# A transformer trunk on one core: the third unit's first two products moved ahead of those that read S2, and the last token tile's chain written first

## The chip, the cores and the metric

The kernel runs on one core of a Trainium2 chip. The metric is the device time of one execution in microseconds (us). The core has TensorE (PE, matrix products), VectorE (DVE), ScalarE (ACT), GpSimd (POOL) and SyncE (SP), which here only issues transfers. Each engine runs its own instructions in a fixed order; they wait for each other by semaphores.

## The reference

One layer on 1024 tokens of width 1024, in float32:

```python
h    = x @ w_in                              # columns: pool | q | k | v | forget gate
pool = scale * GroupLinear(trailing_mean(u) - u)
attn = forgetting_attention(q, k, v, f)      # 8 heads, causal
x    = layer_norm(ALPHA * x + concat(pool, attn) @ w_out)
hid  = square(relu(x @ w_mlp1))              # 1024 -> 4096
x    = layer_norm(ALPHA * x + hid @ w_mlp2)  # 4096 -> 1024
```

## The kernel before, in words

**Precision.** Every operand of a product is split into a hi part (a cast on ScalarE, L71) and a lo part (VectorE subtracts hi from the source, L72). A product is then three matmuls: hi by hi, hi by lo, lo by hi.

**Stages.** First the projections, the pooling and the attention. Then, for token tiles t = 0 to 7 of 128 tokens, the projection by `w_out` (L743 to L745, two banks of 512 columns), the residual (L750) and the norm (`Norm`, with L513 and L516 as its two passes over the tile and a store of the result, L517). Then w_mlp1 in 16 units of 256 columns, and last w_mlp2 in steps (L918).

**Seven products instead of eight.** The product with w_mlp1 cuts x1 (the norm's output, transposed, [channels, tokens]) into four blocks: A11 and A12 are the two halves of the channels for tokens 0 to 511, A21 and A22 those for tokens 512 to 1023. A Strassen-Winograd scheme needs sums of blocks: S1 = A21 - A22, S2 = S1 - A11, S3 = A11 - A21, S4 = A12 + S2. On the weights' side a unit has B11, B21, and B22, T1 to T4, made of sums. The seven products of a unit are `p1` (A11 by B11), `p2` (A12 by B21), `p6` (S2 by T2), `p5` (S1 by T1), `p7` (S3 by T3), `p3` (S4 by B22) and `p4` (A22 by T4): 12 matmuls each (L575), four channel tiles by three hi/lo pairs.

**Where the blocks come from.** `x1_transposed(t, y)` turns one token tile: eight transposes on TensorE (L551). For t below 4 it splits straight into A11 and A12 and keeps a raw copy in `R0[j]`, j = t % 4. For t of 4 and more it makes the differences: ScalarE copies A22, VectorE subtracts three times (L566, L567, L568), POOL adds (L569). The tile just normed is turned while the next one is projected, so tile 7 is turned after the first unit's products have begun. `block(name, src)` splits all four token tiles of a block into two B tiles.

**A unit's weights.** Two loads of 512 KB from w_mlp1, `load_f` (B11 and B21, L592) and `load_g` (L596). `split_f` makes B11 and B21, `sums` makes T1 to T4 in place, `split_t2`, `split_t14` and `split_t3b` split them. `u1` is a copy of `p1`'s bank (L635), `ra` the sum with `p2` (L642), `rb` made behind `p7` (L658) before `p4` adds on to the same bank. Behind `p4` come ReLU and square, sums of the results (`sa`, `sb`, L673 to L678), their splits (L690, L691) and stores to `hid_dram` (L693, L706, issued by POOL).

**Memory and order.** SBUF tiles come from pools shared by a tag: S has 3 tiles, U 2, B 14, Q 10, A 9. The eight split w_out tiles are B tiles, free when the last projection has read them. PSUM has eight banks in a cycle of tags. A tile that is asked for waits until one of its pool is free. A planner in the language's framework fixes each engine's order ahead of the run: among what it deems ready, what stands first in the text goes first. So the text's order is a priority. The first two units, `first` and `second`, run side by side in an order written out by hand (L760 to L808), and `third` is drawn into it; from there on a loop interleaves one unit with the one before it.

Of the kernel before, what the change touches and what calls it, by code (L numbers as in the profile page):

```python
# [8 lines left out]
F32 = mybir.dt.float32  # L9
# [3 lines left out]
ALU = mybir.AluOpType  # L13

P = 128
S = 1024
D = 1024
NT = S // P
# [18 lines left out]
def trunk(ctx, tc, xT, xn, wuqk, wvf, bf, poolw, pscale, wout, g1, b1, w1, w2, g2, b2, out):  # L37
# [5 lines left out]
    nc = tc.nc  # L43
# [7 lines left out]
    def slot(tag, shape, dt=F32R):  # L51
        uid[0] += 1
        return sb.tile([P] + list(shape), dt, tag=tag, bufs=NBUF[tag], name=f"{tag}{uid[0]}")
# [9 lines left out]
    def bank(tag=None):  # L63
        uid[0] += 1
        if tag is None:
            tag = CYCLE[rr[0] % 8]
            rr[0] += 1
        return ps.tile([P, CH], F32, tag=tag, bufs=PBUF[tag], name=f"{tag}{uid[0]}")

    def split(hi, lo, src):  # L70
        nc.scalar.copy(hi, src)  # L71
        nc.vector.tensor_tensor(lo, src, hi.bitcast(F32), ALU.subtract)  # L72
# [8 lines left out]
    def three(dst, a, b, first, last):  # L81

        nc.tensor.matmul(dst, a[0], b[0], start=first, stop=False)  # L83
        nc.tensor.matmul(dst, a[0], b[1], start=False, stop=False)  # L84
        nc.tensor.matmul(dst, a[1], b[0], start=False, stop=last)  # L85
# [97 lines left out]
    for t in range(4, NT):  # L183
        for half in range(2):
            b = bank()[:, 0:VW]
# [273 lines left out]
    H = KT // 2  # L459
# [78 lines left out]
    R0, R1, A22, raw22 = {}, {}, {}, {}  # L538

    def split_to(blk, j, src):  # L540
        js = slice(j * P, (j + 1) * P)
        hi, lo = (a[:, :, js] for a in A[blk])
        split(hi, lo, src)

    def x1_transposed(t, y):
        j = t % 4
        tps = []
        for half in range(2):
            tp = bank()
            for k in range(4):  # L550
                nc.tensor.transpose(tp[:, k * P : (k + 1) * P], y[:, (4 * half + k) * P : (4 * half + k + 1) * P], ident)  # L551
            tps.append(tp.rearrange("p (k t) -> p k t", k=4))
        if t < 4:
            R0[j] = slot("A", [2, H, P], F32)
            for half in range(2):
                split_to(("A11", "A12")[half], j, tps[half])
                nc.scalar.copy(R0[j][:, half], tps[half])
            return

        tag = "A" if j < 2 else "Q"  # L560
        R1[j] = r = slot(tag, [2, H, P], F32)
        if j % 2 == 0:
            raw22[j // 2] = slot(tag, [2, H, P], F32)
        A22[j] = a22 = raw22[j // 2][:, j % 2]
        nc.scalar.copy(a22, tps[1])
        nc.vector.tensor_tensor(r[:, 0], R0[j][:, 0], tps[0], ALU.subtract)  # L566
        nc.vector.tensor_tensor(r[:, 1], tps[0], a22, ALU.subtract)  # L567
        nc.vector.tensor_tensor(R0[j][:, 0], r[:, 1], R0[j][:, 0], ALU.subtract)  # L568
        nc.gpsimd.tensor_tensor(R0[j][:, 1], R0[j][:, 1], R0[j][:, 0], ALU.add)  # L569


    def product(dst, b, a, first):
# [10 lines left out]
    class Unit:  # L583
# [19 lines left out]
        def split_f(self, tag="Q"):  # L603
            if tag == "B":
                w = slot("B", [2, 2, H, P])
                hi, lo = w[:, 0], w[:, 1]
            else:
                hi, lo = slot(tag, [2, H, P]), slot(tag, [2, H, P])
            self.keep(("B11", "B21"), hi, lo, self.f)

        def sums(self, eng=None):

            eng = eng or nc.vector
            f, g = self.f, self.g
            self.t2 = slot("U", [H, P], F32)
            eng.tensor_tensor(f[:, 0], f[:, 0], g[:, 0], ALU.add)
            eng.tensor_tensor(self.t2, g[:, 1], f[:, 0], ALU.add)
            eng.tensor_tensor(f[:, 1], self.t2, f[:, 1], ALU.add)
            eng.tensor_tensor(g[:, 0], g[:, 1], g[:, 0], ALU.add)
# [94 lines left out]
    last = None  # L714
    for m in range(4):
        mh = []
        for half in range(2):
            mf = slot("S", [4, 256], F32)
            nc.sync.dma_start(mf, mix_dram[m, :, 4 * half : 4 * half + 4, :])
            if half:  # L720
                rb = slot("S", [NPAIR, 256], F32)
                for e in range(2):
                    rows = rin_dram[e::2, m * 256 : (m + 1) * 256].rearrange("(o p) t -> o p t", o=1)
                    nc.sync.dma_start(rb[e * HD : (e + 1) * HD], rows.to_broadcast([HD, NPAIR, 256]))
                nc.vector.tensor_tensor(mf, mf, rb, ALU.mult)
            hi, lo = slot("Q", [4, 256]), slot("Q", [4, 256])
            split(hi, lo, mf)
            mh.append((hi, lo))
        for t in (2 * m, 2 * m + 1):
            ts_ = slice((t % 2) * P, (t % 2 + 1) * P)  # L730
            xt = slot("A", [D], F32)
            nc.sync.dma_start(xt, xn[t])
            if t == NT - 1:
                for un in units[:2]:
                    un.load_f()
                    un.split_f("B")
                    if un.u == 0:
                        un.load_g()
                        un.sums(nc.gpsimd)
            yp = [bank() for n in range(2)]  # L740
            for n, part in enumerate(yp):
                ns = slice(n * CH, (n + 1) * CH)
                for k in range(KT):  # L743
                    a = mh[k // 4]
                    three(part, (a[0][:, k % 4, ts_], a[1][:, k % 4, ts_]), (wo[k][0][:, ns], wo[k][1][:, ns]), k == 0, k == KT - 1)  # L745
            if last is not None:
                x1_transposed(*last)
            nm = Norm(xt, gam, bet, x1_dram[t])
            for i, c in enumerate(nm.cols):
                nc.vector.scalar_tensor_tensor(xt[:, c], xt[:, c], ALPHA, yp[i], ALU.mult, ALU.add)  # L750
                nm.stats(i)
            nm.on_vector()
            last = (t, xt)

    def block(name, src):
        A[name] = (slot("B", [H, CH]), slot("B", [H, CH]))
        for j in range(4):
            split_to(name, j, src(j))

    first, second, third = units[:3]  # L760
    second.load_g("A")
    for un in (first, second):
        un.p1()
        un.p2()
    x1_transposed(*last)
    block("S2", lambda j: R0[j][:, 0])
    first.split_t2()
    first.split_t14()
    second.sums()
    second.split_t2()  # L770
    first.p6()
    second.p6()
    block("S1", lambda j: R1[j][:, 1])
    block("S3", lambda j: R1[j][:, 0])
    second.split_t14()
    first.p5()
    second.p5()
    third.load_f()
    block("S4", lambda j: R0[j][:, 1])
    first.split_t3b()  # L780
# [2 lines left out]
    first.p7()  # L783
    second.p7()
    first.p3()
    third.split_f()
    third.load_g()
    second.p3()
    third.sums()
    first.p4()  # L790
    first.sums_s()
    third.split_t2()
    third.p1()
    first.out_r()
    third.split_t14()
    first.out_s()
    second.p4()
    third.p2()
    units[3].load_f()
    units[3].split_f()  # L800
    second.sums_s()
# [302 lines left out]
```

## Time and profile before

| | |
|---|---|
| median of 3 runs | 1059.61 us (1059.41 to 1061.12) |
| the profiled execution | 1059.77 us, its span in the trace 1058.0 us |
| granted TensorE clock, mean over the span | 0.991 |
| TensorE busy | 1023.5 us, 97% |
| VectorE, ScalarE, POOL busy | 761.4 us (72%), 513.6 us (49%), 118.9 us (11%) |

Matmuls are pipelined: the length of one in the trace is longer than the distance to the next, and their ends are modelled. So spacing is read from starts. The granted clock is 1.00 at 2.4 GHz and 0.50 at 1.2 GHz. An idle time is put down to the event that came last before the engine went on.

### The profile page before, as it was taken

The page shows a single profiled execution, that of the slowest core. Times are in us where ns is not written, and L with a number is a line of the kernel's source. Part 1 is how long each engine was busy: PE and PEld are TensorE (multiplying, and loading weights), DVE is VectorE, ACT ScalarE, POOL GpSimd, SP SyncE. Part 2 cuts the span into 40 slices and gives each one's busy share as a digit, 9 for nine tenths or more (in the row PEclk, how much of TensorE's full clock was granted, in tenths as well). Part 3 has the DMA queues.
Part 4 walks back from the last instruction along what each step waited for, and adds up shares of the span by engine and source line. Part 5 has one row for each costly group of instructions (what it writes and reads, how often), then busy time and mean ns, then how long its engine had stood idle before and what let it go on. Part 6 is the DMA issues. An engine that isn't in the chain of part 4 may idle for free.

```text
span 1058.0 us, 14056 instructions
## 1 busy us (share of the span) xinstructions
PE 1023.5 (97%) x5006; PEld 846.8 (80%) x5006; DVE 761.4 (72%) x1297; ACT 513.6 (49%) x822; POOL 118.9 (11%) x187
## 2 busy tenths in 40 slices
PE   8999999999989999899999999999899999999994
PEld 8988787888768888688888888888678888888883
DVE  4576677777896898879878788788686576566446
ACT  4423665565773323567676766668431221122053
POOL 0000000000000021112112122120100000000056
PEclk9999999999999999899999999999999999999998
DMA  6303311021446542238757567575799888868673
GB/s 220 103 27 107 98 50 43 19 64 39 135 152 165 180 152 80 76 132 314 273 219 277 222 257 267 214 268 191 288 296 326 281 271 287 274 217 258 196 224 119
DMA packets 111510, 195.28 MB, mean 185 GB/s; under 512 B 9224, under 2 KB 77640, under 8 KB 111440
## 3 DMA queue, kind: packets, MB, share of 16 engines
q1 hardware_dynamic: 95456, 136.19, 39.5%
q0 software_dynamic: 15984, 58.20, 14.2%
q8 instruction: 39, 0.64, 0.2%
q14 instruction: 31, 0.25, 0.1%
HBM read 126.65 MB, written 67.70 MB: 184 GB/s over the span
## 4 chain that ended last, share of the span: by engine, by line
PE 55%; issue 22%; DVE 8%; DMA 6%; POOL 5%; ACT 3%; SPq 0%; POOLq 0%; DVEq 0%; ACTq 0%
PE s L918 14%; PE pv L918 7%; POOL hid_dram L693 4%; PE pv L384 3%; PE mm L85 2%; PE mm L83 2%; DMA S<-rin_dram 2%; PE mm L84 2%; PE s L83 2%; PE s L85 2%; PE s L84 2%; PE mm L918 2%; PE s L575 2%; PE pt L918 2%; PE pt L83 2%
## 5 line engine op out<-in xcount | busy, mean ns | idle before, releaser
L71 ACT CAST B<-S 128x1024 fp32r<-128x1024 f32 (+1 forms) x94 | 80.1, 869 | 177.8 <-DMA S<-in_w_dram 82.8
L918 PE MATMUL s<-B,Q 128*128 128x512 f32 x549 | 134.1, 391 | 2.6 <-DVE rt L505 2.2
L72 DVE TENSOR_TENSOR B<-S,B 128x1024 fp32r<-128x1024 f32 (+1 forms) x94 | 93.5, 1004 | 46.2 <-ACT B L71 46.0
L918 PEld LDWEIGHTS s<-B,Q 128*128 128x128 f32 x549 | 103.3, 189 | 25.4 <-DVE rt L505 2.6
L575 PE MATMUL s<-B,Q 128*128 128x512 f32 x504 | 121.5, 395 | 0.4 <-ACT B L71 0.4
L575 PEld LDWEIGHTS s<-B,Q 128*128 128x128 f32 x504 | 96.0, 191 | 21.4 <-ACT B L71 0.9
L71 ACT CAST Q<-S 128x1024 fp32r<-128x1024 f32 x53 | 55.5, 1050 | 66.9 <-PE s L575 17.2
L72 DVE TENSOR_TENSOR Q<-S,Q 128x1024 fp32r<-128x1024 f32 x53 | 64.6, 1221 | 25.4 <-ACT Q L71 25.2
L575 PE MATMUL mm<-B,Q 128*128 128x512 f32 x324 | 77.6, 389 | 0.0
L693 POOL DMA_DIRECT2D hid_dram<-A x90 | 48.3, 540 | 234.9 <-ACT A L690 198.0
L575 PEld LDWEIGHTS mm<-B,Q 128*128 128x128 f32 x324 | 60.7, 188 | 13.0 <-DVE Q L72 0.4
L575 PE MATMUL pt<-B,Q 128*128 128x512 f32 x288 | 68.7, 389 | 0.0
L918 PE MATMUL pv<-B,Q 128*128 128x512 f32 x273 | 67.2, 390 | 0.0
L384 PE MATMUL pv<-A,B 128*128 128x256 f32 x320 | 61.6, 297 | 4.9 <-ACT A L369 3.3
L384 PEld LDWEIGHTS pv<-A,B 128*128 128x128 f32 x320 | 49.0, 188 | 21.3 <-ACT A L369 10.0
L575 PEld LDWEIGHTS pt<-B,Q 128*128 128x128 f32 x288 | 54.1, 188 | 11.2
L370 DVE TENSOR_TENSOR A<-pt,A 128x512 fp32r<-128x512 f32 (+1 forms) x80 | 49.2, 634 | 16.4 <-ACT A L369 15.8
L918 PEld LDWEIGHTS pv<-B,Q 128*128 128x128 f32 x273 | 51.3, 188 | 10.8
L347 ACT ACTIVATE A<-A,nm 128x128 f32<-128x128 f32 (+3 forms) x64 | 49.7, 777 | 20.7 <-DVE nm L345 20.4
L691 DVE TENSOR_TENSOR A<-A,A 128x1024 f32<-128x1024 f32 x45 | 53.4, 1219 | 0.0
L83 PE MATMUL mm<-B,B 128*128 128x512 f32 x120 | 51.7, 431 | 0.0
L369 ACT CAST A<-pt 128x512 fp32r<-128x512 f32 (+1 forms) x80 | 41.8, 539 | 16.9 <-PE pt L368 16.2
(395 smaller groups left out, 2214.9 us busy)
## 6 DMA issues: line engine op xcount, KB each, us to landing
hid_dram<-A POOLq DMA_DIRECT2D x105, 512.0 KB, 4.1
Q<-hid_dram SPq DMA_DIRECT2D x139, 256.0 KB
S<-in_w_dram SPq DMA_DIRECT2D x63, 512.0 KB
A<-hid_dram SPq DMA_DIRECT2D x41, 256.0 KB
S<-in_wuqk_dram SPq DMA_DIRECT2D x12, 512.0 KB
Q<-hid_dram SPq DMA_DIRECT2D x44, 128.0 KB
A<-ncf_dram SPq DMA_DIRECT2D x8, 512.0 KB
S<-in_wout_dram SPq DMA_DIRECT2D x8, 512.0 KB
```

Of the source, the lines that this page charges most:

```text
L71: nc.scalar.copy(hi, src)
L72: nc.vector.tensor_tensor(lo, src, hi.bitcast(F32), ALU.subtract)
L83: nc.tensor.matmul(dst, a[0], b[0], start=first, stop=False)
L84: nc.tensor.matmul(dst, a[0], b[1], start=False, stop=False)
L85: nc.tensor.matmul(dst, a[1], b[0], start=False, stop=last)
L347: nc.scalar.activation(pt[:, :nk], pt[:, :nk], AF.Exp, bias=nm, scale=-1.0, accum_out=rsum[h][:, i : i + 1])
L370: nc.vector.tensor_tensor(tt[:, 1, ev], tp[:, ev], tt[:, 0, ev].bitcast(F32), ALU.subtract)
L384: nc.tensor.matmul(ov, V[j][:, h].rearrange("p s d -> p (s d)"), tt[:, s, a:b], start=(j == 0 and s == 0), stop=(j == 2 * m + 1 and s == 1),)
L575: nc.tensor.matmul(dst, b[x][:, k], A[a][y][:, k], start=first and k == 0 and i == 0, stop=k == H - 1 and i == 2, skip_group_check=not first,)
L691: nc.vector.tensor_tensor(x, x, hi.bitcast(F32), ALU.subtract)
L693: nc.gpsimd.dma_start(hid_dram[self.u, :, i, AT[name] : AT[name] + 2 * CH], part.rearrange("p q n t -> p (q n t)"))
L918: nc.tensor.matmul(dst, h[:, p_], w[q_], start=first and u == self.us[0] and j == 0, stop=u == self.us[-1] and j == 2, skip_group_check=no ...
```

## The change

`x1_transposed` makes S2 of a tile in `r[:, 0]` from the first difference (L567's) and, for the last tile, splits it right there; S3 goes to `R0[j][:, 0]`. For the last tile the norm now stands in the text ahead of the transposing of tile 6. `third` gets its own early load of its first weight block into a B tile (`early_f`) and a split into another, in place of `split_f` later; `load_f` stays for the sums. The order written out by hand is rearranged: second's `p1`, S2 of three tiles, the turning of tile 7, second's `p2`, then third's `p1` and `p2`, then the products with S2.

```diff
--- before.py
+++ after.py
@@ -563,10 +563,12 @@
             raw22[j // 2] = slot(tag, [2, H, P], F32)
         A22[j] = a22 = raw22[j // 2][:, j % 2]
         nc.scalar.copy(a22, tps[1])
-        nc.vector.tensor_tensor(r[:, 0], R0[j][:, 0], tps[0], ALU.subtract)
         nc.vector.tensor_tensor(r[:, 1], tps[0], a22, ALU.subtract)
-        nc.vector.tensor_tensor(R0[j][:, 0], r[:, 1], R0[j][:, 0], ALU.subtract)
-        nc.gpsimd.tensor_tensor(R0[j][:, 1], R0[j][:, 1], R0[j][:, 0], ALU.add)
+        nc.vector.tensor_tensor(r[:, 0], r[:, 1], R0[j][:, 0], ALU.subtract)
+        if t == NT - 1:
+            split_to("S2", j, r[:, 0])
+        nc.vector.tensor_tensor(R0[j][:, 0], R0[j][:, 0], tps[0], ALU.subtract)
+        nc.gpsimd.tensor_tensor(R0[j][:, 1], R0[j][:, 1], r[:, 0], ALU.add)
 
 
     def product(dst, b, a, first):
@@ -607,6 +609,13 @@
             else:
                 hi, lo = slot(tag, [2, H, P]), slot(tag, [2, H, P])
             self.keep(("B11", "B21"), hi, lo, self.f)
+
+        def early_f(self):
+
+            raw = slot("B", [2, H, P], F32)
+            w = slot("B", [2, 2, H, P])
+            nc.sync.dma_start(raw.rearrange("p b k f -> p (b k) f"), w1[2 * self.u])
+            self.keep(("B11", "B21"), w[:, 0], w[:, 1], raw)
 
         def sums(self, eng=None):
 
@@ -743,38 +752,45 @@
                 for k in range(KT):
                     a = mh[k // 4]
                     three(part, (a[0][:, k % 4, ts_], a[1][:, k % 4, ts_]), (wo[k][0][:, ns], wo[k][1][:, ns]), k == 0, k == KT - 1)
-            if last is not None:
+            if last is not None and t < NT - 1:
                 x1_transposed(*last)
             nm = Norm(xt, gam, bet, x1_dram[t])
             for i, c in enumerate(nm.cols):
                 nc.vector.scalar_tensor_tensor(xt[:, c], xt[:, c], ALPHA, yp[i], ALU.mult, ALU.add)
                 nm.stats(i)
             nm.on_vector()
+            if t == NT - 1:
+                x1_transposed(*last)
             last = (t, xt)
 
-    def block(name, src):
+    def block(name, src, n=4):
         A[name] = (slot("B", [H, CH]), slot("B", [H, CH]))
-        for j in range(4):
+        for j in range(n):
             split_to(name, j, src(j))
 
     first, second, third = units[:3]
     second.load_g("A")
-    for un in (first, second):
-        un.p1()
-        un.p2()
+    third.early_f()
+    first.p1()
+    first.p2()
+    first.split_t2()
+    second.p1()
+
+    block("S2", lambda j: R1[j][:, 0], 3)
     x1_transposed(*last)
-    block("S2", lambda j: R0[j][:, 0])
-    first.split_t2()
-    first.split_t14()
+    second.p2()
+    third.p1()
+    third.p2()
+    first.p6()
     second.sums()
     second.split_t2()
-    first.p6()
     second.p6()
+    first.split_t14()
     block("S1", lambda j: R1[j][:, 1])
-    block("S3", lambda j: R1[j][:, 0])
+    first.p5()
     second.split_t14()
-    first.p5()
     second.p5()
+    block("S3", lambda j: R0[j][:, 0])
     third.load_f()
     block("S4", lambda j: R0[j][:, 1])
     first.split_t3b()
@@ -783,19 +799,16 @@
     first.p7()
     second.p7()
     first.p3()
-    third.split_f()
     third.load_g()
     second.p3()
     third.sums()
     first.p4()
     first.sums_s()
     third.split_t2()
-    third.p1()
     first.out_r()
     third.split_t14()
     first.out_s()
     second.p4()
-    third.p2()
     units[3].load_f()
     units[3].split_f()
     second.sums_s()
```

## Rows read from the trace of the kernel before

**Rows 1.** The page, part 1: busy us (share of the span), instructions.

```profile
PE 1023.5 (97%) x5006; PEld 846.8 (80%) x5006; DVE 761.4 (72%) x1297; ACT 513.6 (49%) x822; POOL 118.9 (11%) x187
```

**Rows 2.** Waits of TensorE, 434 to the end: us in all, times, longest.

```profile
PE mm L918 <- ACT B L71: 2.4, 1, 2.4
...
PE pv L918 <- ACT A L926: 1.5, 1, 1.5
```

**Rows 3.** Waits of TensorE, 360 to 440.

```profile
PE pv L575 <- ACT B L71: 3.7, 1, 3.7
```

**Rows 4.** Windows of 2 us: busy times, granted clock, share and GB/s of DMA.

```profile
430.00:432.00 2.00, 0.00 (x0) 0.00 (x0) 2.00 (x4) 1.53 (x2) 0.00 (x0) 1.00 0.00 0
...
434.00:436.00 2.00, 1.71 (x4) 1.11 (x5) 2.00 (x4) 0.75 (x2) 2.00 (x1) 0.50 0.18 33
```

**Rows 5.** Timeline of TensorE: start, us, engine, line, operation, count, idle before.

```profile
428.31 0.60 PE L551 MATMUL s<-ident,A 128*128 128x128 f32 x4
...
434.29 8.14 PE L575 MATMUL s<-B,Q 128*128 128x512 f32 x24 [0.41 <-ACT B L71]
...
469.50 5.60 PE L575 MATMUL s<-B,Q 128*128 128x512 f32 x24
```

**Rows 6.** The chain that ended last, 355 to 485: start, us, what.

```profile
360.52 3.35 DMA S<-in_w_dram
...
420.30 2.72 PE pt L575 x12
...
444.92 2.97 PE mm L575 x12
```

**Rows 7.** Timeline of VectorE, 364 to 485.

```profile
384.00 0.68 DVE L750 SCALAR_TENSOR_TENSOR A<-A,pt 128x512 f32<-128x512 f32 x1
...
388.84 1.41 DVE L516 SCALAR_TENSOR_TENSOR A<-A,rt,Q 128x512 f32<-128x512 f32 x2
...
417.43 0.68 DVE L750 SCALAR_TENSOR_TENSOR A<-A,pt 128x512 f32<-128x512 f32 x1
...
421.76 2.38 DVE L513 SCALAR_TENSOR_TENSOR A<-A,mv,Q 128x512 f32<-128x512 f32 x2
...
426.17 1.41 DVE L516 SCALAR_TENSOR_TENSOR A<-A,rt,Q 128x512 f32<-128x512 f32 x2
...
433.50 1.22 DVE L72 TENSOR_TENSOR Q<-S,Q 128x1024 fp32r<-128x1024 f32 x1
434.64 0.68 DVE L72 TENSOR_TENSOR B<-A,B 128x512 fp32r<-128x512 f32 x1
```

**Rows 8.** A window of 20 us among the units.

```profile
540.00:560.00 20.00, 20.00 (x90) 16.57 (x89) 16.40 (x21) 13.68 (x17) 4.76 (x10) 1.00 0.67 257
```

**Rows 9.** Timeline of ScalarE, 364 to 485.

```profile
412.41 1.14 ACT L71 CAST B<-A 128x512 fp32r<-128x512 f32 x2 [4.49 <-PE pt L84]
...
465.80 1.05 ACT L690 CAST A<-A 128x1024 fp32r<-128x1024 f32 x1
...
469.72 1.03 ACT L690 CAST A<-A 128x1024 fp32r<-128x1024 f32 x1
```

**Rows 10.** Timeline of SyncE's queue, 340 to 485.

```profile
416.94 0.33 SPq L596 DMA_DIRECT2D A<-in_w_dram  x1
426.94 0.99 SPq L517 DMA_DIRECT2D x_dram<-A  x2
```

**Rows 11.** Timeline of POOL, 364 to 485.

```profile
433.75 5.12 POOL L569 TENSOR_TENSOR A<-A 128x512 f32<-128x512 f32 x1 [10.82 <-DVE A L568]
467.17 0.71 POOL L693 DMA_DIRECT2D hid_dram<-A  x1 [28.30 <-ACT A L690]
```

**Rows 12.** Timeline of VectorE, 484 to 545.

```profile
484.60 0.68 DVE L658 TENSOR_TENSOR A<-Q,s 128x512 f32<-128x512 f32 x1
```

**Rows 13.** A window of 10 us.

```profile
470.00:480.00 10.00, 10.00 (x46) 8.29 (x45) 10.00 (x14) 6.58 (x10) 2.67 (x5) 1.00 0.99 356
```

**Rows 14.** Transfers, 400 to 520: KB each, median us from issue to landing.

```profile
hid_dram<-A POOLq DMA_DIRECT2D x25, 512.0 KB, 4.3
```

## The prediction

> **What bounds the kernel now.** I read the page first [rows 1]: TensorE is busy 97% of the span. At such a share a change pays only where TensorE stands still or runs slowly, so the next view is its waits, and after that the windows of the stage that the diff touches.
>
> Behind the 435th us no wait of TensorE is above 2.4 us, and all are at steps (L918) of a later stage [rows 2]. In the stretch of the change one stands out, 3.7 us on a hi copy of ScalarE (L71) [rows 3]. The 2 us windows show both halves of that hole [rows 4]: no matmul from 430 to 432, and a granted clock of 0.50 from 434 to 436, which is the lower level, 1.2 GHz, although TensorE is busy again. Before the clock fell the engine had stood idle for almost 4 us.
>
> The timeline of TensorE says what is on either side [rows 5]. Four products (`p1` and `p2` of first and second, 12 matmuls each, 2.72 us [rows 6]) run to 428.31, then the eight transposes of the last token tile until about 429.2, then nothing but a lone matmul until 434.29. From there to 469.50, where the third unit's `p6` starts, lie 12 products: `p6 p5 p7 p3 p4` of the first two units and the third's `p1` and `p2`. Counted: 12 x 2.72 = 32.6, and 0.9 for the transposes, is 33.5; the stretch from 428.31 to 469.50 took 41.2. The excess is 7.7 us. It is made of the idle part (429.2 to 434.29, less one matmul of 0.23: 4.9), of 24 matmuls in 8.14 instead of 2 x 2.72 (2.7), and of 0.25 in second's `p5`, 2.97 instead of 2.72.
>
> What is late at 434.29 is S2 of the last tile. Its chain in VectorE's timeline [rows 7]: the norm's end (the L516 pair from 426.17), transposes, then L566, L567 and L568 in a queue without a gap (VectorE is busy 2.00 of 2 in [rows 4]), a cast on ScalarE, and the lo half at 434.64, behind T1 and T4 of the first unit (433.50, 1.14 us).
>
> **Does the time later on follow this stage?** From 480 to about 740 TensorE is busy 20.00 of 20 in every window; one stands in [rows 8]. A unit is 7 products, 19.04 us, and its loads wait for tiles that products free. I take it that a gain of TensorE at 434 is carried to the end whole.
>
> **The change, part by part.**
>
> *Third's `p1` and `p2` ahead of `p6`.* No matmul is added; 24 move from among the `p4` products to ahead of first's `p6`: 5.4 us of work for the hole. Laid out at 2.72 a product: the projection of tile 7 ends at 416.5, transposes of tile 6 to 417.3, first `p1`, `p2`, second `p1` to 425.5, transposes of tile 7 to 426.4, second `p2` to 429.1, third `p1` to 431.8, `p2` to 434.6, then `p6`. So S2 may come as late as 434.6 at no cost. Even if the stretch from the transposes' end (429.2) to the lo half (434.64 + 0.60 = 435.2) stays at its old 6.0 us, S2 is there at 432.4, 2.2 us early. If the transposes were put behind second's `p2`, it would be there at 436.0: 1.4 lost. I take 0.
>
> *The last norm ahead of tile 6's differences.* The transposes of tile 7 can't start before the norm is done: 425.5 in this layout. Before, the L516 pair ended at 427.5, since splits, L566 to L568 and sums went in between and the L513 pair took 2.38. Tile 3's norm ran from 384.00 to 390.2 (388.84 + 1.33) with two splits in it, 1.2 us [rows 7]: about 5.0 alone. From 417.43 that is 422.4. Ends: 422.4 and 427.5; the second would hold TensorE 2.0 us. I take the first: 0.
>
> *S2 from the difference itself.* The same three subtractions, one cast and one lo split; S2 now needs two of the three subtractions, 0.6 less on the chain. POOL's addition waits for `r[:, 0]`; it feeds S4, first wanted at 450.9.
>
> *Third's early weights.* Added: one load of 512 KB (the same w1 block comes again for the sums) and two B tiles. The split of 1024 columns moves from behind first's `p3` to before 429.1. The first w_out tile comes free at 412.41, when ScalarE's next cast into a B tile was released [rows 9]. SP issues second's G at 416.94 [rows 10]; in front of it or behind it the load goes by 417.3, and takes 3.35 as another w1 load did [rows 6]: 420.7, with cast and lo half (1.05 and 1.2) 423, 6 us early. Behind the norm's store, which goes at about 422.4 with a 5.0 us norm, it would still be split by 429. What SP holds behind it, second's G, is read for a T2 that is wanted at 437.3. The price is 0.
>
> *B tiles.* Two of the eight w_out tiles go to the new pair, so S4 waits for the tiles of units (422.8, 429.1) and A22 for the third's (434.6); `p3` wants S4 at 450.9 and `p4` wants A22 at 456.4. Nothing lost.
>
> *VectorE's queue.* The engine without gaps keeps its work. Until first's `p5` at 440.0 it must do, from 417.4: the norm 5.0; 17 operations of 512 columns, 0.60 apart (six differences, two lo halves of S2 and two of S1, three L642, two sums, two T2); two splits of 1024, 1.14 each (third's early one, T1/T4): 17.5 of 22.6 us. In the same way I count 19.2 of 25.4 to second's `p5`, 23.4 of 28.1 to first's `p7` and 28.1 of 33.5 to first's `p3`. It fits, but a ready operation can stand behind another. T1/T4 of second waited for Q tiles that `p6` frees; this cost the 0.25 above and I leave it in.
>
> POOL's additions disturb this: beside one the L513 pair took 2.38, where the L516 pair of the same width took 1.41 [rows 7], and the addition itself 5.12 when VectorE's queue was full [rows 11]. The Trainium skill (GPSIMD Engine Reference, 1. Specifications) says that the two engines share SBUF interfaces and that VectorE operations with two SBUF inputs contend. These rows agree in part: the lo half at 434.64 ran in its 0.60 beside the 5.12 us addition. By that rule the last S2 half could stretch; by the rows 1.0 us is the worst, inside the 2.2 us early above.
>
> *The sum.* 7.7 returned, less 0.25 for second's `p5` and 0.25, an estimate of the same kind, for one more wait in VectorE's queue: 7.2. The profiled execution took 1059.77, 1.77 over its span and 0.16 over the median 1059.61. 1059.77 - 7.2 = 1052.6; less 0.16, 1052.4.
>
> **Rivals.**
>
> *1. A part is handed back at third's `p4`.* Third's `p1` and `p2` also covered the time after first's `p4`. From the end of that product (461.3) to third's `p4` (469.50 + 7 x 2.72 = 488.5) lay 27.2 us; now 21.8. `p4` writes over what L658 has read, at 484.60 + 0.69 = 485.3 [rows 12], 24.0 after 461.3. With the same queue in between `p4` waits 2.2. For it: VectorE at 10.00 of 10 from 470 to 480 [rows 13]. Against it: third's L642, T2, T1/T4 and the next unit's split (0.6 + 0.6 + 1.14 + 1.14 = 3.5) can be done before, since third's early split needs no Q tiles. Time: 7.2 - 2.2, 1054.6.
>
> *2. The transposes stay late.* The norm ends at 427.5 after all, in a fixed order of TensorE: 2.0 lost, 1054.4. For it: the queue is as full as it was. Against: the 5.0 of tile 3.
>
> *3. The change only moves the hole.* Were the new load behind a store that leaves as before (426.94 [rows 10]), it would land at 431.3, be split at 433.6, and third's `p1` would wait 4.5 from 429.1, as long as the old hole, with the low clock's 2.7: 0.5 gained, 1059.1. Against: the norm is done earlier too, and this queue had second's G ahead of that store.
>
> *4. Slower: A tiles.* There are nine. At the third copy, 469.72 [rows 9], I count nine in use: `ra`, `sa`, `sb` of first, `ra`, `rb` of second, four copies on their way out. Third's `ra` was taken behind third's `p2`, after 469.5; now it is held from 434.6 on. An output that finds no tile waits for a store: cast 465.80, issue 467.17 [rows 9, 11], 4.3 to land [rows 14], 5.7 in all, and VectorE's queue stands behind it. One such wait on TensorE's path with the clock falling (5.7 + 2.7 = 8.4) cancels the gain; the second decides it: 14.1, 1066.5. Against: TensorE has other products ahead of `p4`, and four tiles are free again within one cycle.
>
> **How the numbers follow.** Chances: my forecast 0.64 (own range 1051.4 to 1053.5), rival 1 0.19, rival 2 0.07, rival 3 0.05, rival 4 0.05. The measurement can tell 0.2%, 2.1 us. The forecast and rivals 1 and 2 lie below 1057.5: 0.90 faster; rival 3 within: 0.05; rival 4 slower: 0.05. The range reaches up over rivals 1 and 2 and both at once: 7.2 - 2.0 - 2.2 = 3.0 gained, 1056.6. Down, 7.7 returned and the 1.5 us wait of [rows 2] gone in a new order give 1050.4; I stop at 1050.8.
>
> **What the changed profile would show.** Right: TensorE without an idle window between 417 and 480, the clock at 1.00 throughout, transposes of the last tile at about 425.5, 24 matmuls of third ahead of first's `p6`, third's `p6` at about 462, and every later row some 7 us earlier. Rival 1 shows as a wait of TensorE on L658 or a split near 480; rival 2 as one on L516; rival 3 as one on third's first split; rival 4 as VectorE waiting on a store. The prediction is wrong if units come further apart than 19.04, or if the waits at L918 grow.

## The result, and the profile after

The changed kernel took 1063.07 us (median of 21 runs, 1059.22 to 1066.55), the kernel before 1059.44 in 21 runs beside it: a ratio of 1.0031 [1.0022, 1.0039]. It is slower by 0.3%, where 0.7% faster was forecast. The profiled execution took 1061.9 us, its span 1060.1. In the changed file the matmuls of the products are L577 (L575 before), the copy of `p6`'s bank L656 (L647), the operation that frees the bank of `p4` L667 (L658), the output's splits L699 and L700 (L690, L691), the last stage's products L931 (L918).

First the waits of TensorE, from 400 to the end: engine, tile and line, releaser, us in all, times, longest.

```profile
PE s L577 <- ACT Q L71: 2.8, 2, 1.6
PE mm L931 <- ACT B L71: 2.6, 1, 2.6
...
PE pv L577 <- DVE A L667: 1.4, 1, 1.4
PE s L577 <- DVE Q L72: 1.0, 1, 1.0
...
```

The 3.7 us wait for S2 [rows 3] is gone. In its place TensorE waits for Q tiles. A block of x1 is a B tile; a Q tile as the operand of a product is a split weight, here T2, T1 or T4. So what is late now is on the weights' side. The timeline of TensorE says where:

```profile
425.85 0.60 PE L551 MATMUL mm<-ident,A 128*128 128x128 f32 x4
...
429.48 2.88 PE L577 MATMUL pv<-B,B 128*128 128x512 f32 x12
...
434.92 2.88 PE L577 MATMUL s<-B,Q 128*128 128x512 f32 x12
438.99 0.73 PE L577 MATMUL s<-B,Q 128*128 128x512 f32 x2 [1.19 <-ACT Q L71]
440.76 2.59 PE L577 MATMUL s<-B,Q 128*128 128x512 f32 x10 [1.03 <-DVE Q L72]
444.97 0.73 PE L577 MATMUL s<-B,Q 128*128 128x512 f32 x2 [1.62 <-ACT Q L71]
445.92 0.53 PE L577 MATMUL pt<-B,Q 128*128 128x512 f32 x1 [0.22 <-ACT Q L71]
446.26 4.11 PE L577 MATMUL s<-B,Q 128*128 128x512 f32 x10
...
469.02 2.88 PE L577 MATMUL pv<-B,Q 128*128 128x512 f32 x12
...
485.34 2.88 PE L577 MATMUL mm<-B,Q 128*128 128x512 f32 x12
489.64 3.02 PE L577 MATMUL pv<-B,Q 128*128 128x512 f32 x12 [1.41 <-DVE A L667]
```

Up to 434.92 it goes as laid out: the last tile's transposes at 425.85, third's `p1` and `p2` at 429.48 and 432.19, first's `p6` at 434.92 without a wait. Then second's `p6` stops twice, at its hi matmuls (438.99) and at its lo ones (440.76), and the `p5` products twice more (444.97, 445.92). Ten matmuls from 446.26 then take until 450.21, 3.95 instead of 10 x 0.227 = 2.27. From 434.92 to third's `p6` at 469.02 lie 10 products, 27.2 us at 2.72 each; they took 34.1. The new hole is 6.9 us, the old one was 7.7. Third's `p4` starts late as well: 489.64, against 485.34 + 2.72, is 1.6 us; in the kernel before it started at 488.54 without a wait. Together that is 8.5 against 7.7, and accounts for most of the 1.0 us by which the stage measured below grew. The windows of 10 us show that the hole lies further back (PE busy, then the other engines; the clock and the DMA share stand near the end):

```profile
430.00:440.00 10.00, 8.53 (x37) 6.42 (x35) 10.00 (x17) 6.08 (x12) 1.30 (x1) 1.00 0.00 0
440.00:450.00 10.00, 7.40 (x23) 5.29 (x24) 8.95 (x12) 5.38 (x7) 0.00 (x0) 0.83 0.27 91
```

The clock of 0.83 from 440 to 450 is full speed with a piece at the lower level, 1.2 GHz, behind the stops, as in [rows 4]: in windows of 2 us it is 0.57 from 446 to 448, 0.58 from 448 to 450, and 1.00 on both sides. VectorE, without a gap until 440, looks like the bound. ScalarE's timeline says otherwise:

```profile
416.26 1.05 ACT L71 CAST B<-B 128x1024 fp32r<-128x1024 f32 x1 [9.02 <-DMA B<-in_w_dram]
...
437.83 0.59 ACT L656 COPY Q<-s 128x512 f32<-128x512 f32 x1 [2.72 <-PE s L577]
438.32 0.62 ACT L71 CAST Q<-U 128x512 fp32r<-128x512 f32 x1
...
443.38 0.59 ACT L656 COPY Q<-s 128x512 f32<-128x512 f32 x1 [2.37 <-PE s L577]
443.87 2.94 ACT L71 CAST Q<-S 128x1024 fp32r<-128x1024 f32 x3
```

And VectorE's:

```profile
433.41 0.68 DVE L626 TENSOR_TENSOR U<-A,S 128x512 f32<-128x512 f32 x1
...
436.42 3.69 DVE L72 TENSOR_TENSOR B<-A,B 128x512 fp32r<-128x512 f32 x6
440.03 0.68 DVE L72 TENSOR_TENSOR Q<-U,Q 128x512 fp32r<-128x512 f32 x1
...
480.49 0.69 DVE L683 TENSOR_TENSOR A<-A 128x512 f32<-128x512 f32 x1 [1.45 <-DMA hid_dram<-A]
...
488.90 0.68 DVE L667 TENSOR_TENSOR A<-Q,pv 128x512 f32<-128x512 f32 x1
```

Second's T2 is summed by 434.1 (L626). Its hi cast (Q<-U) comes only at 438.32: in ScalarE's order it stands behind the copy of first's `p6` bank, and that copy waits 2.72 us, idle, for `p6` to end. The lo half follows at 440.03 and `p6` goes on at 440.76. The cast had ended at 438.94; for the last 1.1 us the lo half stood behind VectorE's row of six other lo halves (436.42), so VectorE's queue has a part in the second stop. Then the same again: the hi casts of first's T1 and T4 (443.87) stand behind the copy of second's `p6` bank, for which ScalarE waits 2.37. The diff shows why. Before, `split_t2` of second and `split_t14` of first stood ahead of first's `p6`. After, `sums` and `split_t2` of second stand behind first's `p6`, and `split_t14` of first behind second's `p6`. The text's order is the priority, so each cast was put behind a copy that can't run before the product ahead of it has ended.

**Theory O (order):** those two places cost the hole. **Rivals:** V, VectorE is simply full in this stretch; L, ScalarE's 9.02 us wait for third's early load (416.26) pushed everything later; A, the early `p1` and `p2` hold tiles that others need, the prediction's fourth rival.

### The profile page after: what moved, and what is told of

It reads as the page before. It is cut to its first block, busy times and chain, and to the rows that moved or that the text cites. A ratio compares the mean times of both kernels' runs of the same rounds, so it can differ in the third digit from the quotient of the medians.

```text
span 1060.1 us, 14061 instructions
## 1 busy us (share of the span) xinstructions
PE 1025.0 (97%) x5006; PEld 846.8 (80%) x5006; DVE 759.1 (72%) x1297; ACT 513.0 (48%) x822; POOL 114.7 (11%) x187
## 4 chain that ended last, share of the span: by engine, by line
PE 57%; issue 22%; DVE 8%; DMA 5%; POOL 5%; ACT 3%; SPq 0%; POOLq 0%; DVEq 0%; ACTq 0%
PE s L931 15%; PE pv L931 8%; POOL hid_dram L702 4%; PE pv L384 3%; PE mm L85 2%; PE mm L83 2%; PE mm L84 2%; PE s L85 2%; PE s L83 2%; PE s L84 2%; PE pt L931 2%; PE s L577 2%; DVE B L72 2%; PE pt L83 2%; PE pt L368 2%
## 5 line engine op out<-in xcount | busy, mean ns | idle before, releaser
L931 PE MATMUL s<-B,Q 128*128 128x512 f32 x549 | 134.8, 393 | 2.3 <-DVE rt L505 2.2
L931 PEld LDWEIGHTS s<-B,Q 128*128 128x128 f32 x549 | 103.7, 189 | 25.1 <-DVE rt L505 2.6
L577 PE MATMUL s<-B,Q 128*128 128x512 f32 x480 | 116.1, 394 | 3.8 <-ACT Q L71 2.8
L577 PEld LDWEIGHTS s<-B,Q 128*128 128x128 f32 x480 | 91.0, 190 | 24.1 <-ACT Q L71 3.7
L577 PE MATMUL pt<-B,Q 128*128 128x512 f32 x300 | 71.9, 389 | 0.2 <-ACT Q L71 0.2
L577 PE MATMUL mm<-B,Q 128*128 128x512 f32 x300 | 71.6, 389 | 0.0
L931 PE MATMUL pv<-B,Q 128*128 128x512 f32 x273 | 67.2, 390 | 0.0
L577 PEld LDWEIGHTS pt<-B,Q 128*128 128x128 f32 x300 | 56.3, 188 | 12.3 <-ACT Q L71 0.7
L577 PEld LDWEIGHTS mm<-B,Q 128*128 128x128 f32 x300 | 56.3, 188 | 11.7
L931 PEld LDWEIGHTS pv<-B,Q 128*128 128x128 f32 x273 | 51.2, 188 | 11.2 <-DVE A L941 0.2
L700 DVE TENSOR_TENSOR A<-A,A 128x1024 f32<-128x1024 f32 x45 | 53.5, 1218 | 0.2
```

Source lines behind the costliest of these rows:

```text
L577: nc.tensor.matmul(dst, b[x][:, k], A[a][y][:, k], start=first and k == 0 and i == 0, stop=k == H - 1 and i == 2, skip_group_check=not first,)
L700: nc.vector.tensor_tensor(x, x, hi.bitcast(F32), ALU.subtract)
L931: nc.tensor.matmul(dst, h[:, p_], w[q_], start=first and u == self.us[0] and j == 0, stop=u == self.us[-1] and j == 2, skip_group_check=no ...
```

## The experiments

Whole times spread by some us between executions, also ahead of and behind the stage, so beside the ratio stands the length of the stage in the profiled execution: from tile 6's transposes (L551) to the copy of the last unit's `p6` bank. Before: 416.52 to 717.53, 301.0. After: 416.78 to 718.77, 302.0. Without any hole it would be 301.0 - 7.7 = 293.3. Each stage is read from one execution; the changed kernel's two profiles differ by 1.4 us.

| run | stage us | median us | before beside it | ratio |
|---|---|---|---|---|
| e1_t2_first | 296.4 | 1055.79 | 1060.1 | 0.9964 [0.9953, 0.9976] |
| e2_split_later | 302.3 | 1062.79 | 1060.1 | 1.0025 [1.001, 1.004] |
| e3_both | 296.9 | 1056.25 | 1060.1 | 0.9967 [0.9956, 0.9979] |
| e4_chain_only | 298.5 | 1057.53 | 1060.1 | 0.9976 [0.9965, 0.9988] |
| e0_again | 303.4 | 1061.88 | 1059.78 | 1.0014 [1.0003, 1.0025] |
| e7_t2_only | 300.2 | 1060.0 | 1059.78 | 1.0004 [0.9991, 1.0017] |
| e6_p2_late | 296.1 | 1055.2 | 1059.78 | 0.9957 [0.9945, 0.9969] |
| e5_third_only | 300.9 | 1059.75 | 1059.78 | 1.0007 [0.9998, 1.0016] |
| e12_t14_only | 298.2 | 1057.86 | 1059.58 | 0.9986 [0.9976, 0.9995] |
| e9_hold_a_tile | 296.2 | 1054.87 | 1059.58 | 0.9962 [0.9951, 0.9973] |
| e8_best | 296.5 | 1056.96 | 1059.58 | 0.9972 [0.996, 0.9984] |

**e1_t2_first: second's sums and T2 split and first's T1/T4 split ahead of first's `p6`, all else as changed.**

```diff
+    second.sums()
+    second.split_t2()
+    first.split_t14()
     first.p6()
-    second.sums()
-    second.split_t2()
     second.p6()
-    first.split_t14()
```

> The changed kernel with three lines moved up: second's sums and T2 split and first's T1/T4 split stand ahead of first's p6 in the text instead of behind p6. Theory (order): in the changed kernel the hole came back because ScalarE's casts of second's T2 and first's T1/T4 stand in its order behind the copies of p6's bank, so that they can't start before p6 is through (437.8 and 443.4). With the lines moved, the two waits of TensorE between 437 and 447 (some 7 us with the half clock) go: about 1055 to 1057, 6 to 7 below the changed kernel, as long as third's p4 doesn't take more than its 1.4. Rival (VectorE is full): the engine is busy 20.00 of 20 from 420 to 440, so whatever is put first pushes something else behind TensorE's need, S2 or S1 most likely: no more than 1.5 below the changed kernel, 1061.5 to 1063, with the wait at another split.

It became faster than both kernels, 0.9964. ScalarE's timeline now has the casts ahead of the copy:

```profile
435.65 0.62 ACT L71 CAST Q<-U 128x512 fp32r<-128x512 f32 x1 [1.09 <-DVE U L626]
436.18 1.04 ACT L71 CAST Q<-S 128x1024 fp32r<-128x1024 f32 x1
...
439.37 0.59 ACT L656 COPY Q<-s 128x512 f32<-128x512 f32 x1 [1.62 <-PE s L577]
```

TensorE's timeline has three products without a stop, and two short waits left:

```profile
436.45 8.32 PE L577 MATMUL s<-B,Q 128*128 128x512 f32 x36
...
445.77 2.56 PE L577 MATMUL pt<-B,Q 128*128 128x512 f32 x10 [0.55 <-DVE Q L72]
...
480.83 2.88 PE L577 MATMUL mm<-B,Q 128*128 128x512 f32 x12
485.57 3.01 PE L577 MATMUL pv<-B,Q 128*128 128x512 f32 x12 [1.86 <-DVE A L667]
```

VectorE was busier than in the changed kernel, and the clock stayed whole:

```profile
430.00:440.00 10.00, 10.00 (x46) 8.28 (x45) 10.00 (x16) 5.78 (x11) 1.30 (x1) 1.00 0.00 1
440.00:450.00 10.00, 9.45 (x43) 7.49 (x42) 10.00 (x16) 8.10 (x13) 0.00 (x0) 1.00 0.45 139
```

That is the verdict on V: a VectorE at 10.00 of 10 up to 450 costs TensorE 0.55 us there. Theory O holds for this stretch; the 1.86 us at 485.57 are another matter, taken up below.

**e2_split_later and e3_both: is ScalarE's wait for the early load the cause?** In e2 the load stays where it is and third's early split moves behind the turning of tile 7; e3 is e1 and e2 together.

```diff
     x1_transposed(*last)
+    third.early_split()
     second.p2()
```

> The changed kernel with third's early split standing behind the turning of tile 7 in the text; the load stays where it is. Theory (order): ScalarE no longer stands 9.0 us at the head of its queue for the load, so the splits of S2 and S1 for the first tiles run at 413 to 417, where VectorE was idle for 3.6 us; but T2 and T1/T4 still stand behind p6's copies, so TensorE's waits at 438 to 447 stay: at most 1 below the changed kernel, 1062 to 1063. Rival (VectorE is full): the 3.6 us of work taken out of the full stretch shortens the waits by as much: 1059 to 1060.

> Both edits, T2 and T1/T4 ahead of p6 and third's split behind the turning of tile 7. Theory (order): about the same as with the first edit alone, at best 1 lower: 1054 to 1057. Rival (VectorE is full): the two add up, and only both together bring it under 1058.

e2 stayed slow (1.0025), with TensorE's waits as in the changed kernel, 2.8 and 1.1 us on Q tiles; e3 was not better than e1. L falls: in e2 two casts went ahead of that wait (415.10, released by TensorE after 5.64 us), ScalarE then waited 2.26 us for the load instead of 9.02, and no time was gained by it. That these casts were not wanted earlier is the likely reason; it was not tested by itself.

**e4_chain_only and e5_third_only: the two halves of the change on the kernel before.** e4 has the shorter chain (norm first, S2 from the difference, tile 7 turned behind second's `p1`) and leaves third and the splits as they were. e5 has third's early load, `p1` and `p2`, and leaves the chain.

```diff
     x1_transposed(*last)
+    third.p1()
+    third.p2()
     block("S2", lambda j: R0[j][:, 0])
```

> The kernel before with one part of the change: S2 from the first difference, the last norm ahead of tile 6's differences, tile 7 turned ahead of second's p2. Third's products and weights stay where they were, and T2 and T1/T4 ahead of p6. Theory (order): no cover is added, so the hole shortens only by what the chain comes earlier: S2 of the last tile 2 to 3 us earlier, the clock may still fall; 1055 to 1058. Rival (VectorE is full): the chain gains nothing, because the same work has to pass ahead of it: 1059 to 1060, as before.

> The kernel before with the other part of the change alone: third's early load and its p1 and p2 right behind the turning of tile 7; S2 made and split as before, the norm where it was, T2 and T1/T4 ahead of p6. Theory (order): this has the cover without the bad order, so it should gain about as the first edit did: 1054 to 1057. Rival (VectorE is full, S2's chain is the limit): S2 of the last tile comes at the same distance from the turning as before, 6.0 us, and the cover is 5.4 us: the hole shrinks to about 1 and the clock stays up: 1054 to 1056; if third's split goes ahead of S2 on VectorE, 1057 to 1059.

The chain alone gains 0.24%. Waits of 0.7 and 1.0 us for S2 are left, and a slow piece behind them (granted clock 0.50 from 434 to 436). The cover alone gains nothing, although it is 5.4 us of work: two waits for S2 stay, and the clock falls behind them (34 matmuls from 438.70 to 448.08 are 9.38 us instead of 7.7; granted clock 0.65 from 438 to 440 and 0.50 from 440 to 442). TensorE in e5:

```profile
436.55 0.73 PE L575 MATMUL s<-B,Q 128*128 128x512 f32 x2 [1.57 <-ACT B L71]
438.70 9.54 PE L575 MATMUL s<-B,Q 128*128 128x512 f32 x34 [1.42 <-DVE B L72]
...
488.44 3.06 PE L575 MATMUL pv<-B,Q 128*128 128x512 f32 x12 [1.66 <-DVE A L665]
```

Two things ate the cover. S2 of the last tile came later than before, its last lo half in VectorE's timeline of e5 at

```profile
437.97 0.68 DVE L72 TENSOR_TENSOR B<-A,B 128x512 fp32r<-128x512 f32 x1
```

against 434.64 [rows 7]: 9.2 us from the transposes' end to the end of this lo half, where it had been 6.0. Two L649 sums (432.14, 433.94), which the kernel before had done by 430.6, and an L624 of 1.77 us (436.28) stood ahead of it. And third's `p4` waits 1.66 us for L665, where the kernel before had no wait. By starts, the hole of e5 is 5.6 us and `p4` is 1.8 late: together 7.4, the old 7.7 but for 0.3.

So the two halves aren't a sum: cover is worth something only where S2 comes within it, and it has a price at third's `p4`.

**e0_again: the changed kernel once more.**

> The changed kernel once more, for a second profile and median beside the edits of this call. Both theories: 1.0022 to 1.0039 of the kernel before, TensorE's waits at second's p6 and at p5 again, and a wait of 1 to 2 at third's p4.

Again slower, by less: 1.0014 [1.0003, 1.0025]. Its four waits are those of the first profile, but the slow piece began one product earlier, and a second followed:

```profile
440.26 0.73 PE L577 MATMUL s<-B,Q 128*128 128x512 f32 x2 [1.19 <-ACT Q L71]
442.07 3.88 PE L577 MATMUL s<-B,Q 128*128 128x512 f32 x10 [1.07 <-DVE Q L72]
447.57 0.73 PE L577 MATMUL s<-B,Q 128*128 128x512 f32 x2 [1.62 <-ACT Q L71]
...
449.11 3.69 PE L577 MATMUL s<-B,Q 128*128 128x512 f32 x10
```

**e7_t2_only and e12_t14_only: which of the moved splits?** e7 moves only second's `sums` and `split_t2` ahead of first's `p6`, e12 only first's `split_t14`.

```diff
+    first.split_t14()     # e12; in e7: second.sums(), second.split_t2()
     first.p6()
```

> The changed kernel with second's sums and T2 split ahead of first's p6, but first's T1/T4 split still behind second's p6. Theory (order): the waits at second's p6 (1.2 and 1.0 in the profile) go, the wait for T1/T4 behind the copy of second's bank stays: 2 to 3 below the changed kernel, 1060 to 1061, and the other 4 to 5 us of the gain of the first edit belong to T1/T4 and the half clock that follows it. Rival: the two waits are one shortage of VectorE, so moving one alone gives either all or nothing.

> The changed kernel with first's T1/T4 split alone ahead of first's p6; second's sums and T2 split stay behind it. With the run that moved T2 alone, this makes the four corners of the first edit. Theory (order): the wait for T2 behind the copy of first's bank stays (1.2 and 1.0, TensorE then at its higher level), the wait for T1/T4 and the half clock behind it go: 1057.5 to 1058.5. Rival (VectorE is full): T1/T4's lo half then takes 1.1 us ahead of T2's, so the wait for T2 grows by as much: 1059 to 1060.

T2 alone takes both stops out of second's `p6`, but the stop at `p5` stays, and the slow piece with it. TensorE in e7:

```profile
435.48 5.60 PE L577 MATMUL s<-B,Q 128*128 128x512 f32 x24
442.70 0.73 PE L577 MATMUL s<-B,Q 128*128 128x512 f32 x2 [1.62 <-ACT Q L71]
444.16 0.65 PE L577 MATMUL pt<-B,Q 128*128 128x512 f32 x1 [0.73 <-ACT Q L71]
444.86 3.90 PE L577 MATMUL s<-B,Q 128*128 128x512 f32 x10
```

In e12 T2's cast is as late as in the changed kernel (behind the copy, at 439.21), and yet second's `p6` waits little. Two short waits follow at second's `p5`, and the clock stays at 1.00 from 430 to 460:

```profile
435.81 5.39 PE L577 MATMUL s<-B,Q 128*128 128x512 f32 x23
441.60 3.24 PE L577 MATMUL s<-B,Q 128*128 128x512 f32 x13 [0.40 <-DVE Q L72]
445.78 0.73 PE L577 MATMUL pt<-B,Q 128*128 128x512 f32 x2 [0.94 <-ACT Q L71]
447.04 2.55 PE L577 MATMUL pt<-B,Q 128*128 128x512 f32 x10 [0.53 <-DVE Q L72]
```

The reason for the little wait is in the order that the planner wrote: with T1 and T4 split early, 7 of the 12 matmuls of first's `p5` stand ahead of second's `p6`, and 2 more ahead of its lo matmuls. They cover T2's wait. So first's T1 and T4, whose raw sums lay ready long before, were the larger part: 3.8 us of the stage against 1.8 for T2, and 5.6 for both, in one profile of each run.

**e6_p2_late, e9_hold_a_tile: the wait at third's `p4` that e1 leaves.** In e1 third's `p4` starts 2.0 us late (485.57, against 480.83 + 2.72). It waits for L667, which stands in a VectorE queue without gaps behind L683, and that waited for a store. e6 puts third's `p2` back behind second's `p4`. e9 is e1 with one A tile more held, a dummy with one column written, from third's `p2` until the copy of the fourth unit's `p6` bank; the dummy is no part of what is computed.

```diff
-    third.p1()
-    third.p2()
+    third.p1()
...
     second.p4()
+    third.p2()
```

> T2 and T1/T4 ahead of p6 as in the first edit, and third's p2 back behind second's p4, so that only p1 stands ahead of p6 and third's ra takes its A tile late. Theory (A tiles): the 1.9 us wait at third's p4 comes from second's sb waiting 1.8 for a store to free an A tile, since third's ra holds one from 438 on; it goes, and one product less of cover costs at most 1: 1054 to 1055.5. Rival (cover): what p2 early takes from the time behind first's p4 makes VectorE late there whatever the tiles do; then p2 late removes the wait as well, but VectorE shows no wait on a store in either, and p6 now waits 2 or more for S2 or T2: 1056 to 1057.

> The first edit (T2 and T1/T4 ahead of p6) with one A tile more taken out of use: an empty A tile is held from third's p2 until the fourth unit's first copy behind p6 (some 436 to 486), so eight are left; the work is the same but for two tiny operations on POOL and ScalarE. Theory (A tiles): the wait of VectorE and ScalarE on stores between 470 and 480 grows, and with it TensorE's wait at third's p4, from 1.9 to 4 to 7: 1058 to 1062. Rival (VectorE's load): the wait at third's p4 is a matter of how much VectorE has to do behind first's p4, and stays within 0.5: 1055.5 to 1056.5.

In e6 the wait halved; the stage is only 0.3 us shorter than e1's. TensorE and, from VectorE's timeline, the waits for stores:

```profile
487.14 3.01 PE L577 MATMUL pv<-B,Q 128*128 128x512 f32 x12 [0.92 <-DVE A L667]
```

```profile
475.09 0.69 DVE L682 TENSOR_TENSOR A<-A,A 128x512 f32<-128x512 f32 x1 [0.45 <-DMA hid_dram<-A]
476.28 0.69 DVE L683 TENSOR_TENSOR A<-A 128x512 f32<-128x512 f32 x1 [0.50 <-DMA hid_dram<-A]
...
486.41 0.68 DVE L667 TENSOR_TENSOR A<-Q,pv 128x512 f32<-128x512 f32 x1
```

VectorE's wait for the store (first number) is as long as TensorE's at `p4` (second) in three kernels (changed: 1.45 and 1.41; e1: 1.79 and 1.86; e12: 1.79 and 1.80). But e9, which should have made it longer, did not come out so: VectorE waited 2.03 and 0.56 for stores, TensorE only 0.69 and 0.66, and the time was e1's. The extra tile also changed the order of the products there (another product went ahead of third's `p4`), so it was no clean test. That the early products cost something at `p4` is shown by e5, which gives this wait to the kernel before, and by e6, which halves it; that they do so by the A tiles alone is not.

**e8_best: e6 with second's T1 and T4 early as well.** S1 and `second.split_t14` go ahead of second's `p6`.

```diff
     first.p6()
+    block("S1", lambda j: R1[j][:, 1])
+    second.split_t14()
     second.p6()
-    block("S1", lambda j: R1[j][:, 1])
     first.p5()
-    second.split_t14()
     second.p5()
```

> T2 and T1/T4 ahead of p6, third's p2 behind second's p4, and second's T1/T4 split ahead of second's p6 as well. Theory (order): what is left of the waits at p6 and p5 (0.4 and what VectorE's 4.9 us row of S3 and S4 splits ahead of second's T1/T4 cost) goes, 0.3 to 0.8 below the run with p2 late: 1054.3 to 1055. Rival: the split takes Q tiles that the copies of p6's banks want, and p5 waits instead: 1055.5 to 1057.

Its stage is e6's within 0.4 us, with much the same two waits (0.4 and 1.1, in e6 0.4 and 0.9), so this edit gains nothing at that place. Of the versions run, e6 has the lowest ratio, 0.9957; e1, e3, e8 and e9 can't be told from it by their intervals.

## Why the prediction was wrong

**The bound and the old hole: right.** TensorE's waits decided. The hole of 7.7 us was of the size and at the place said, and it went. One of its parts is read from a length: by starts (434.29 to 442.27) the 24 slow matmuls lost 2.5, not 2.7, and with 2.5 the parts add up to 7.7.

**Third's `p1` and `p2` as cover, the last norm first, S2 from the difference: right.** Transposes at 425.85 (said 425.5), first's `p6` at 434.92 (434.6), S2's last lo half done at 431.38 + 0.90 = 432.3 (432.4), though it was stretched beside a POOL addition (430.43, 1.30 us). The norm ended at 426.0, not at 422.4, since splits and differences still went in between; TensorE was busy until 425.85, so this cost nothing. e5 adds what the prediction had not said. It took the cover to work even if S2 stayed 6.0 us behind the transposes; without the shorter chain that became 9.2, and the cover gained nothing.

**Third's early weights, "the price is 0": right in the time.** The load was issued at 412.66, ahead of second's G, and its cast went at 416.26. That ScalarE would stand 9 us for it was not seen, but in e2 and e3 nothing was gained by shortening that wait.

**The step that failed is the one on VectorE's queue.** It counted the work to be done by each due time, 17.5 of 22.6 us, and booked 0.25 + 0.25 for operations that stand behind another. Two things were wrong in it. It counted VectorE alone, while each lo half follows a cast on ScalarE, and ScalarE's place in the order was not looked up. And the change part by part left out two of the moves in the diff: the sums and T2 of second behind first's `p6`, T1 and T4 of first behind second's; the count had this work in it, but not its place. Where 0.25 + 0.25 was booked, the new hole took 6.9. Measured by e1, these places cost 302.0 - 296.4 = 5.6 us of the stage, and 0.5 to 0.7% of the time: 1.0014 or 1.0031 becomes 0.9964. The first sign was in the text: a split written behind a product gets a lower priority than that product's copy, and the copy is an instruction that waits for TensorE.

The Trainium skill says in a sentence (Perfetto Trace Analysis, Tensor Engine Instruction) that ScalarE and VectorE are strict in their order, where TensorE has a limited reorder of its weight loads. The rows agree: the cast's source was there at 434.1 and ScalarE was idle for 2.72 us, and it did not go ahead of the copy.

**The rivals.** The first, a wait at third's `p4`, is there: 1.6 us late in the changed kernel, 1.8 in e5 and 2.0 in e1, where 2.2 was worked out. The forecast put it at nothing, since 3.5 us of VectorE's work could be done before; that was its second error, and 2.0 of the 3.1 us by which e1's stage is above 293.3. The fourth, A tiles, showed its sign, VectorE waiting for a store (1.45 us at L683; the kernel before has no such wait from 462 to 492), but not its size of 5.7 and the low clock; how much of the wait at `p4` is due to it is not separated. The second did not happen. The third had the outcome nearest to what came, a hole that only moves, by another mechanism than the load it named: it asked only whether the new operands come in time, not whether the old ones still do.

**What stays open.** The stage is 1.0 us longer than before in the first profile, and 303.4 against 301.0 in e0_again's, while the medians differ by 3.6 (21 runs) and 2.1 (e0_again). In the first profile 0.9 of the span's 2.1 lies behind the stage. TensorE's longest wait there is 2.6 us, at L931 near 757, and [rows 2] have 2.4 at that place. It comes and goes with no edit aimed at it: in e1 no more than 0.2 us is left of it, and e8 has 2.8 (granted clock 0.66 from 750 to 760). Behind the stage e1 is 1.9 us shorter than the changed kernel and e8 1.6 longer than e6. So a part of what the ratios say beyond the stage comes from there. No run was made for it, and its cause is not shown.

## What to carry to other kernels

When work is moved up to cover a late operand, list every operand of the products behind it, with the engine and the place in the order of each step that makes it; a queue of which only the load is counted says nothing on what stands at its head. Preparations for the next product belong ahead of the current product's own copy in the text, since that copy waits for TensorE and blocks all that is behind it. And test the halves alone: here the cover was worth 0, the shorter chain 0.24%, both with the splits in their place 0.36%. The last two intervals overlap; the stages, 298.5 and 296.4, set them 2.1 us apart.

## What the runs showed of the hardware

The same four waits of TensorE, equal within 0.04 us in two profiles of one kernel, were followed by one slow piece at 446.26 in the first (granted clock 0.83 from 440 to 450) and by two in the other (442.07 and 449.11; 0.75). The cost of a row of short stops is thus not fixed from one execution to the next: 302.0 and 303.4 us of stage.

Beside POOL's addition a VectorE subtraction with both inputs in SBUF took 1.8 times as long. POOL in the changed kernel, then VectorE:

```profile
422.88 1.29 POOL L571 TENSOR_TENSOR A<-A,Q 128x512 f32<-128x512 f32 x1 [12.31 <-DVE Q L567]
```

```profile
422.81 0.68 DVE L570 TENSOR_TENSOR A<-A,pv 128x512 f32<-128x512 f32 x1
...
423.48 1.25 DVE L72 TENSOR_TENSOR B<-A,B 128x512 fp32r<-128x512 f32 x1
...
425.98 0.68 DVE L72 TENSOR_TENSOR B<-A,B 128x512 fp32r<-128x512 f32 x1
```

The lo half that began inside the 1.29 us took 1.25, the next one 0.68. L570, which has one input in PSUM (pv), ran beside the same addition in 0.68. The L513 pair, now clear of POOL, took 1.41 instead of 2.38 [rows 7]. In the kernel before, the lo half at 434.64 kept its 0.60 and the addition beside it was the one that stretched, 5.12 us [rows 11] against 1.29 here. The rule of the Trainium skill that the prediction weighed (GPSIMD Engine Reference, 1. Specifications: shared SBUF interfaces, contention with two SBUF inputs) agrees with these rows; either engine was the one held up.
